# Row-factor products placed later, its low half in another pool, keys' root seeded on ScalarE, decay rows in fewer writes: an encoder trunk on one core

## The chip, the cores and the metric

One of a Trainium2 chip's cores runs the whole kernel in one launch. The metric is device time in microseconds (us), the median of several runs; lower is better. TensorE (PE) multiplies matrices into PSUM banks, VectorE (DVE) and ScalarE (ACT) work on tiles of 128 partitions, GpSimd (POOL) does a few additions, and SyncE (SP) issues the DMAs.

## The reference, cut to what matters

The reference is a bidirectional encoder trunk of two layers on 512 tokens of 1024 features:

```python
for i in range(DEPTH):                                   # DEPTH = 2
    h = h + 0.5 * swiglu(rmsnorm(h, ffn1_norm[i]), ffn1_w_gu[i], ffn1_w_down[i])
    hn = rmsnorm(h, mix_norm[i])
    if i % N_MIXERS == 0: h = h + ssd_mixer(hn, ...)     # state-space mixer, two directions
    else:                 h = h + neighbourhood_attention(hn, ...)
    h = h + 0.5 * swiglu(rmsnorm(h, ffn2_norm[i]), ffn2_w_gu[i], ffn2_w_down[i])
    gate = jax.nn.sigmoid(rmsnorm(h, ple_norm[i]) @ ple_w_gate[i])
    h = h + gate * rmsnorm(p[i] @ ple_w_proj[i], ple_post_norm[i])
```

`rmsnorm(x, g)` is `x * rsqrt(mean(x*x) + 1e-6) * g`; its row factor, the `rsqrt`, is one number per token. `swiglu` has 2816 hidden features (22 tiles of 128), the attention has 16 heads of 64 with a root mean square of each head's query and key, and the mixer has 32 heads with decays that are running sums along the tokens.

## The kernel before, in words

Activations lie transposed, features on the partitions and the 512 tokens along the free axis, so `h` is 8 tiles of 128x512. Every operand is split into a rounded high part and the remainder, and a product of two tiles is three matmuls: L282 (high weight, high activation), L285 (high weight, low activation), L286 (low weight, high activation). I call the three matmuls of one 128-row tile of the contraction a pair; a gemm over 1024 features is 8 pairs, that is 24 matmuls of 512 columns. The later part of each feed-forward (FFN) stage uses blocks of seven products on half tiles, 256 columns wide (L501 to L503); `sums` prepares their inputs from the normalised activations, on DVE and ACT.

Weights arrive in the order of one list: SP loads a unit into a `wr` buffer (L208, 4 buffers), ACT casts the high part (L225, `wh`, 3 buffers), DVE subtracts for the low part (L227, `wl`, 3 buffers). `unit()` hands out one that is ready and prepares the list's next. `ahead(norm)` prepares four more entries behind the row factor's low half.

A norm runs beside the gemm that needs it. `Norm.prep` splits `h[k]` times the gain without the row factor, since that is one number per token and can be applied to the gemm's result. Meanwhile ACT squares `h[k]` (L332) and POOL or DVE adds the squares (L336). `SumSq.begin` then makes the row factor: a high part of the sum (L341, ACT) and a low part (L342, DVE), both from the pool `sq` of 4 buffers; two matmuls of 128x512 with a constant matrix, the wide products (L345, L346), which add over the partitions and spread the sum; logarithm, exponential and square on ACT (L348 to L350), the first two each with an ACT_TABLE_LOAD; and one Newton step on DVE (L351, L352), whose result R lies in the pool `rt` of 3 buffers. There are eleven such places. In the FFN of the first layer's first half (`first`), R is begun between two plain gemms; in each second FFN (FFN2) `side_by_side` runs gate and up of f = 0 together, holding back pair 7 of both, and `begin` stands after pair 4 of up (`at=4`); in the second layer's first FFN it stands behind both gemms (`at=8`). Before R is used, the next gate gemm runs four pairs (`c = 4`). When R is there, DVE forms gate times R (L433) and up times R (L436), ACT takes Silu (L434), DVE multiplies (L437), and `sums` begins with h times R (L455).

The mixer's front computes decay rows on PE, copies them (L727) and their exponentials (L728) to one tile, and SP writes them to DRAM as `crow` and `vrow`: 8 DMAs each of 32x128, in turn (L731, L732). From `crow` one head's row is read back to all partitions (`hs<-crow`, L790), ACT makes its decay matrix from it (L793, L796), and behind that on ACT stand the convolution's copies (L745) that DVE goes on with (L749).

In attention the keys' root (8x512, one row per head of a half) is computed twice, near and far, by `newton_rsqrt` on DVE: 2 integer operations and 3 times 3 others (L317 to L323). DVE also adds the bias to scores (L1274) and takes maxima (L1277); PE turns the result over (L1298) and multiplies it with the values (L1307).

The order of the instructions on each engine is fixed when the program is built: a scheduler takes them mostly in program order by what they need, and `issue_after` ties some behind others.

Of the kernel before, what the change touches and what calls it, by code (L numbers as in the profile page):

```python
# [70 lines left out]
def trunk(ctx, tc, A, out):  # L71
# [30 lines left out]
    def xa(dt=F32R):  # L102
        return md(dt)

    def rt():
        return bp.tile([P, T], F32, name=nm("rt"), tag="rt", bufs=3)

    def bank(tag, bufs):
        return ps.tile([P, T], F32, name=nm("ps"), tag=tag, bufs=bufs)
# [176 lines left out]
            gemm.last = te.matmul(out=pt, lhsT=lo[:, sl], rhs=part(xp, 0, cols), start=False,  # L286
                                  stop=last and k == n - 1)

    def side_by_side(pts, pairs, mid=None, at=4):

        ws = [unit() for _ in pts]
        k = len(pairs) - 1
        for pt, w in zip(pts, ws):
            c = min(at, k) if mid and pt is pts[-1] else k
            gemm(pt, w, pairs[:c], last=False)
            if mid and pt is pts[-1] and at <= k:
                mid()
            if c < k:
                gemm(pt, w, pairs[c:k], first=False, last=False, off=c)
        for pt, w in zip(pts, ws):  # L300
            gemm(pt, w, pairs[k:], first=False, off=k)
        if mid and at > k:
            mid()

# [10 lines left out]
    def newton_rsqrt(m, y, a):  # L315
# [7 lines left out]
            last = v.scalar_tensor_tensor(out=y, in0=a, scalar=1.5, in1=y, op0=ALU.add, op1=ALU.mult)  # L323
        return last

    class SumSq:
        def __init__(self):
            self.acc = None
# [8 lines left out]

        def begin(self, scale=1.0, eps=EPS):

            hi, lo = sq(F32R), sq(F32R)  # L340
            s.copy(out=hi, in_=self.acc)  # L341
            self.last = v.scalar_tensor_tensor(out=lo, in0=self.acc, scalar=eps * D / (scale * P), in1=hi,  # L342
                                               op0=ALU.add, op1=ALU.subtract)
            pt = px_bank()
            te.matmul(out=pt, lhsT=mean[scale], rhs=hi, start=True, stop=False)  # L345
            te.matmul(out=pt, lhsT=mean[scale], rhs=lo, start=False, stop=True)  # L346
            y, a = rt(), self.acc
            s.activation(out=y, in_=pt, func=AF.Ln)  # L348
            s.activation(out=y, in_=y, func=AF.Exp, scale=-0.5)
            s.activation(out=a, in_=y, func=AF.Square)  # L350
            v.scalar_tensor_tensor(out=a, in0=a, scalar=-0.5, in1=pt, op0=ALU.mult, op1=ALU.mult)  # L351
            v.scalar_tensor_tensor(out=y, in0=a, scalar=1.5, in1=y, op0=ALU.add, op1=ALU.mult)  # L352
            self.y = y

        def end(self):
            return self.y
# [1 line left out]
    class Norm:  # L358
# [18 lines left out]
        def begin(self, half=False):  # L377
            if half:
                self.ss.begin(4.0, 4.0 * EPS)
            else:  # L380
                self.ss.begin()

        def end(self):
            return self.ss.end()


    def ffn(norm, nxt, between=None, first=None, at=4):
# [9 lines left out]
        def gate_up(f):  # L397
            pg = mm_bank()
            if not (first and R[0] is None and f == 2):
                pu = mm_bank()  # L400
            if first and f < 2:
                held.append((f, pg, pu))
                if f == 1:
                    first([p for x in held for p in x[1:]], norm.pairs)
                    mid()
                return
            if f == 0 and not first:
                side_by_side((pg, pu), norm.pairs, mid, at)
                held.append((f, pg, pu))
                return  # L410
            if R[0] is None:

                w, c = unit(), 4
                gemm(pg, w, norm.pairs[:c], last=False)
                R[0] = norm.end()
                gemm(pg, w, norm.pairs[c:], first=False, off=c)
                while held:
                    activate(*held.pop(0))
                sums(left.pop(0))
                if first:  # L420
# [126 lines left out]
        for what, *a in ffn_order(chunks):  # L547
            if what == "plain":
                if left and R[0] is not None:
                    sums(left.pop(0))  # L550
                gate_up(a[0])
            elif what == "block":

                if between and a in ([chunks[-1][0] // 2, 0], [NF // 2 - 1, 4]):
                    next(between)
                block(*a)
            elif what == "between":
                made = between and next(between)
            else:
                c, d = a  # L560
                last = c == len(chunks) - 1
                pt = mm_bank() if last else px_bank()
                gemm(pt, unit(last and d == KD - 1), [mids[f] for f in range(*chunks[c])])
                v.scalar_tensor_tensor(out=h[d], in0=pt, scalar=0.5, in1=h[d], op0=ALU.mult, op1=ALU.add)
                if last:
                    nxt(d)
                    if d in (2, 4) and made is not None:
                        made[d // 2]()
        return made and made[0]


    def ple_proj(l):
# [27 lines left out]
            for n in range(KD):  # L600
                pp[n] = (pp[n], r3)

        yield pp, (lambda: ss.begin(4.0, 4.0 * EPS)), finish

    def ple(l, norm, pp, nxt):
        halves = (slice(0, T // 2), slice(T // 2, T))
# [15 lines left out]
        for n in range(KD):  # L622
# [7 lines left out]
                    (sy, s)[x].dma_start(out=out[:, n, cs], in_=h[n][:, cs])  # L630
                continue
            pt = mm_bank()
            gemm(pt, unit(n == KD - 1), norm.pairs, behind=n == 0)
            if n == 0:
                norm.begin(half=True)
                held = pt
# [10 lines left out]
    def ssd(norm, nxt):  # L647
# [11 lines left out]
        gemm(ptd, unit(), norm.pairs)  # L659
        norm.begin()  # L660
        pt0, w0 = mm_bank(), unit()
        gemm(pt0, w0, norm.pairs[:5], last=False)
        R = norm.end()
        gemm(pt0, w0, norm.pairs[5:], first=False, off=5)

        keep = md()
        dtk = keep[:, 0, :].rearrange("p (c k) -> p c k", c=NC)
# [10 lines left out]
        for k in range(KD):  # L678
            t = t2()
            v.scalar_tensor_tensor(out=t, in0=hk[k], scalar=col(norm.gain + k), in1=R, op0=ALU.mult, op1=ALU.mult)  # L680
            xn.append(md(F32R))
            split(xn[k], t, None)

        def steps():

# [43 lines left out]
            for dr in range(2):  # L729
                for c in range(NC):  # L730
                    sy.dma_start(out=crow[dr, :, c * P:(c + 1) * P], in_=rowt[c * 32:(c + 1) * 32, dr * P:(dr + 1) * P])  # L731
                    sy.dma_start(out=vrow[dr, :, c * P:(c + 1) * P],  # L732
                                 in_=rowt[c * 32:(c + 1) * 32, 256 + dr * P:256 + (dr + 1) * P])

        ydram = dp.tile([16, P, T], F32, name="ydram")
        ss = SumSq()
# [292 lines left out]

        for i, cur in enumerate(project(0)):  # L1030
            if i == 2:
                steps()
        e0 = [expo(0, 0)]

        def count(gi, i):
            if gi == NG - 1:
# [42 lines left out]
        ss.begin(0.5, 4.0 * EPS)  # L1079
        for d in range(KD):  # L1080
            pt, w = mm_bank(), unit(d == KD - 1)
            gemm(pt, w, prs[:4], last=False)
            if d == 0:
                r2 = ss.end()
            old = sc()
            sy.dma_start(out=old, in_=hd[d])
            gemm(pt, w, prs[4:], first=False, off=4)

            h[d] = hs()
            u = t2()  # L1090
# [17 lines left out]
    def attention(norm, nxt):  # L1108
# [24 lines left out]
        def keys(js):  # L1133
# [3 lines left out]
            for j in js:  # L1137
# [9 lines left out]
                if j == 2:  # L1147

                    w = unit()
                    gemm(pt, w, norm.pairs[:4], last=False)  # L1150
                    R = norm.end()
                    gemm(pt, w, norm.pairs[4:], first=False, off=4)
                else:
                    gemm(pt, unit(), norm.pairs)
                if j == 4:
# [21 lines left out]
                m, rk, ra = sc(), sc(), sc()  # L1177
                v.tensor_scalar(out=m[:8], in0=kst[:8], scalar1=EPS, scalar2=None, op0=ALU.add)
            yield
            newton_rsqrt(m[:8], rk[:8], ra[:8])  # L1180
            rkd = dp.tile([8, T], F32, name=nm("rkd"))
            sy.dma_start(out=rkd, in_=rk[:8])
            yield
# [376 lines left out]
```

## Time and profile before

| | before |
|---|---|
| median of 3 runs | 2300.32 us (2300.14 to 2300.46) |
| profiled execution | 2300.35 us |
| its span | 2298.5 us, so 1.85 us lie around it |
| PE busy | 2280.6 us, 99% |
| DVE busy | 1829.9 us, 80% |
| ACT busy | 1228.2 us, 53% |
| granted TensorE clock | 1.0 |

A row of the timeline gives start, duration, engine, source line, operation, output and inputs, shape and count; in brackets stands how long the engine sat idle before it and what ended that. Ends of matmuls are modelled: those of 512 columns show some 0.39 us each, but start about 0.23 us apart, so PE loses time wherever two starts lie farther apart than that; the bracket shows about 0.16 us less than is lost. The stages in the trace, from the rows of their lines: first FFN 0 to 360 us, mixer to 893, second FFN to 1257, gated embedding to 1306; in the second layer first FFN to 1645, attention to 1890, second FFN to 2253, embedding to 2298.

### The profile page before, as it was taken

The page shows a single profiled execution, that of the slowest core. Times are in us where ns is not written, and L with a number is a line of the kernel's source. Part 1 is how long each engine was busy: PE and PEld are TensorE (multiplying, and loading weights), DVE is VectorE, ACT ScalarE, POOL GpSimd, SP SyncE. Part 2 cuts the span into 40 slices and gives each one's busy share as a digit, 9 for nine tenths or more (in the row PEclk, how much of TensorE's full clock was granted, in tenths as well). Part 3 has the DMA queues.
Part 4 walks back from the last instruction along what each step waited for, and adds up shares of the span by engine and source line. Part 5 has one row for each costly group of instructions (what it writes and reads, how often), then busy time and mean ns, then how long its engine had stood idle before and what let it go on. Part 6 is the DMA issues. An engine that isn't in the chain of part 4 may idle for free.

```text
span 2298.5 us, 35082 instructions
## 1 busy us (share of the span) xinstructions
PE 2280.6 (99%) x13578; PEld 2008.7 (87%) x13578; DVE 1829.9 (80%) x2522; ACT 1228.2 (53%) x2098; POOL 322.2 (14%) x261
## 2 busy tenths in 40 slices
PE   9999999999999999999999999999999999999999
PEld 7999997888888888899998789999878888999987
DVE  8878868887878959987875897887578869878856
ACT  6433445777677775444446544444546755444453
POOL 0000001355555641000003100000120010000020
PEclk9999999999999999999999999999999999999999
DMA  5323323444444543323223222232557732333222
GB/s 194 116 75 110 106 81 126 161 155 139 144 140 147 186 167 120 106 97 103 88 89 108 101 101 97 92 106 77 168 178 221 228 113 91 111 106 101 82 81 90
DMA packets 105223, 281.68 MB, mean 123 GB/s; under 512 B 13136, under 2 KB 14032, under 8 KB 105056
## 3 DMA queue, kind: packets, MB, share of 16 engines
q1 hardware_dynamic: 104768, 279.30, 36.7%
q8 instruction: 106, 1.74, 0.3%
q14 instruction: 61, 0.50, 0.1%
q10 hardware_dynamic: 288, 0.14, 0.0%
HBM read 259.70 MB, written 13.40 MB: 119 GB/s over the span
## 4 chain that ended last, share of the span: by engine, by line
PE 89%; DVE 6%; ACT 2%; issue 1%; DMA 1%; SPq 0%; POOL 0%; DVEq 0%; POOLq 0%; ACTq 0%
PE ps L282 17%; PE ps L286 17%; PE ps L285 17%; PE ps L503 10%; PE ps L502 10%; PE ps L501 10%; DVE wl L227 1%; PE ps L923 1%; PE ps L882 1%; PE ps L1264 1%; PE ps L903 1%; PE ps L1318 1%; PE ps L838 1%; PE ps L827 1%; ACT wh L225 1%
## 5 line engine op out<-in xcount | busy, mean ns | idle before, releaser
L282 PE MATMUL ps<-md,wh 128*128 128x512 f32 (+1 forms) x2032 | 796.8, 392 | 1.7 <-DVE t L749 1.6
L286 PE MATMUL ps<-md,wl 128*128 128x512 f32 (+1 forms) x2032 | 790.5, 389 | 3.1 <-DVE wl L227 3.1
L285 PE MATMUL ps<-md,wh 128*128 128x512 f32 (+1 forms) x2032 | 791.3, 390 | 0.3 <-DVE md L311 0.3
L225 ACT CAST wh<-wr 128x1024 fp32r<-128x1024 f32 (+2 forms) x395 | 351.4, 892 | 425.8 <-PE ps L285 234.5
L227 DVE TENSOR_TENSOR wl<-wr,wh 128x1024 fp32r<-128x1024 f32 (+2 forms) x395 | 418.5, 1062 | 90.9 <-ACT wh L225 88.3
L286 PEld LDWEIGHTS ps<-md,wl 128*128 128x128 f32 x2032 | 381.5, 188 | 86.2 <-DVE wl L227 6.1
L282 PEld LDWEIGHTS ps<-md,wh 128*128 128x128 f32 x2032 | 382.2, 188 | 76.6 <-issue 2.4
L285 PEld LDWEIGHTS ps<-md,wh 128*128 128x128 f32 x2032 | 382.3, 188 | 73.2 <-DVE md L311 1.0
L225 ACT CAST wh<-md 128x1024 fp32r<-128x1024 f32 x175 | 183.5, 1049 | 318.1 <-PE ps L502 300.4
L336 POOL TENSOR_TENSOR sq<-sq,sq 128x512 f32<-128x512 f32 x71 | 98.9, 1393 | 1635.2 <-ACT sq L332 1315.6
L502 PE MATMUL ps<-md,wh 128*128 128x256 f32 x980 | 277.4, 283 | 0.8 <-DVE md L465 0.8
L501 PE MATMUL ps<-sc,wh 128*128 128x256 f32 x980 | 276.9, 283 | 0.8 <-ACT wh L225 0.8
L503 PE MATMUL ps<-sc,wl 128*128 128x256 f32 x980 | 277.4, 283 | 0.1
L503 PE MATMUL ps<-md,wl 128*128 128x256 f32 x980 | 277.3, 283 | 0.0
L502 PE MATMUL ps<-sc,wh 128*128 128x256 f32 x980 | 277.3, 283 | 0.0
L501 PE MATMUL ps<-md,wh 128*128 128x256 f32 x980 | 277.2, 283 | 0.0
L507 DVE TENSOR_TENSOR t<-ps,t 128x512 f32<-128x512 f32 x245 | 165.8, 689 | 137.7 <-PE ps L503 137.2
L227 DVE TENSOR_TENSOR wl<-md,wh 128x1024 fp32r<-128x1024 f32 x175 | 213.4, 1220 | 16.2 <-ACT wh L225 16.1
L501 PEld LDWEIGHTS ps<-sc,wh 128*128 128x128 f32 x980 | 187.7, 192 | 4.8 <-ACT wh L225 1.0
L502 PEld LDWEIGHTS ps<-sc,wh 128*128 128x128 f32 x980 | 187.7, 192 | 3.8
L502 PEld LDWEIGHTS ps<-md,wh 128*128 128x128 f32 x980 | 188.0, 192 | 2.2 <-DVE md L465 1.0
L501 PEld LDWEIGHTS ps<-md,wh 128*128 128x128 f32 x980 | 188.0, 192 | 1.2
(217 smaller groups left out, 2916.8 us busy)
## 6 DMA issues: line engine op xcount, KB each, us to landing
wr<-in_w_gw_dram SPq DMA_DIRECT2D x70, 512.0 KB, 3.6
md<-in_w_gw_dram SPq DMA_DIRECT2D x70, 512.0 KB, 4.6
wr<-in_w_in_dram SPq DMA_DIRECT2D x65, 512.0 KB, 3.5
wr<-in_w_dn_dram SPq DMA_DIRECT2D x128, 256.0 KB, 2.6
wr<-in_w_gu_dram SPq DMA_DIRECT2D x32, 512.0 KB, 3.5
hs<-crow SPq DMA_DIRECT2D x64, 256.0 KB, 3.7
wr<-in_w_dn_dram SPq DMA_DIRECT2D x32, 384.0 KB, 3.1
wr<-in_w_qkv_dram SPq DMA_DIRECT2D x24, 512.0 KB, 3.6
```

The lines of the kernel that those rows point to most:

```text
L225: splits.append(s.copy(out=hi[:, :n], in_=raw[:, :n]))
L227: v.tensor_sub(out=lo[:, :n], in0=raw[:, :n], in1=hi[:, :n])
L282: m = te.matmul(out=pt, lhsT=hi[:, sl], rhs=part(xp, 0, cols), start=first and k == 0, stop=False)
L285: te.matmul(out=pt, lhsT=hi[:, sl], rhs=part(xp, 1, cols), start=False, stop=False)
L286: gemm.last = te.matmul(out=pt, lhsT=lo[:, sl], rhs=part(xp, 0, cols), start=False, stop=last and k == n - 1)
L336: (v if fast else g).tensor_add(out=self.acc, in0=self.acc, in1=q)
L501: te.matmul(out=o, lhsT=hi[:, sl], rhs=xh, start=j == 0 and kk == 0, stop=False)
L502: te.matmul(out=o, lhsT=hi[:, sl], rhs=xl, start=False, stop=False)
L503: te.matmul(out=o, lhsT=lo[:, sl], rhs=xh, start=False, stop=j == 1 and kk == 3)
L507: v.tensor_add(out=k[to], in0=pt, in1=k[other])
L827: te.transpose(out=pt[:, cs(i)], in_=src[:, cs(c)], identity=ident)
L838: te.matmul(out=pt[:, cs(c)], lhsT=bt[:, dr, cs(c)], rhs=ct_[:, dr, cs(c)], start=True, stop=True)
```

## The change

`SumSq.begin` now makes only the two halves of the sum, and the low half takes a buffer of `rt` instead of `sq`. The two wide products and all behind them become a step of its own, `spread`, which callers place. The root's five instructions become a helper, `seeded_rsqrt`, which the keys' root now uses too, in place of `newton_rsqrt`. The decay rows go out in 4 DMAs of 32x2x128 for `crow` and 4 for `vrow`, all of `crow` first. In the mixer's front one weight split is taken up at k = 5 of the loop over the normalised tiles.

```diff
-    def side_by_side(pts, pairs, mid=None, at=4):
+    def side_by_side(pts, pairs, mid=None, at=4, then=None):
...
         for pt, w in zip(pts, ws):
             gemm(pt, w, pairs[k:], first=False, off=k)
+            if then and pt is pts[0] and at <= k:
+                then()
...
+    def seeded_rsqrt(m, y, a):
+
+        s.activation(out=y, in_=m, func=AF.Ln)
+        s.activation(out=y, in_=y, func=AF.Exp, scale=-0.5)
+        s.activation(out=a, in_=y, func=AF.Square)
+        v.scalar_tensor_tensor(out=a, in0=a, scalar=-0.5, in1=m, op0=ALU.mult, op1=ALU.mult)
+        v.scalar_tensor_tensor(out=y, in0=a, scalar=1.5, in1=y, op0=ALU.add, op1=ALU.mult)
...
-            hi, lo = sq(F32R), sq(F32R)
-            s.copy(out=hi, in_=self.acc)
-            self.last = v.scalar_tensor_tensor(out=lo, in0=self.acc, scalar=eps * D / (scale * P), in1=hi,
+            self.scale, self.hi, self.lo = scale, sq(F32R), rt(F32R)
+            s.copy(out=self.hi, in_=self.acc)
+            self.last = v.scalar_tensor_tensor(out=self.lo, in0=self.acc, scalar=eps * D / (scale * P), in1=self.hi,
                                                op0=ALU.add, op1=ALU.subtract)
+
+        def spread(self):
+
             pt = px_bank()
-            te.matmul(out=pt, lhsT=mean[scale], rhs=hi, start=True, stop=False)
-            te.matmul(out=pt, lhsT=mean[scale], rhs=lo, start=False, stop=True)
...
+            for k, x in enumerate((self.hi, self.lo)):
+                te.matmul(out=pt, lhsT=mean[self.scale], rhs=x, start=k == 0, stop=k == 1)
+            self.y = rt()
+            seeded_rsqrt(pt, self.y, self.acc)
...
-                side_by_side((pg, pu), norm.pairs, mid, at)
+                side_by_side((pg, pu), norm.pairs, mid, at, norm.spread)
...
-                w, c = unit(), 4
+                w, c = unit(), 1
                 gemm(pg, w, norm.pairs[:c], last=False)
+                if first or at > len(norm.pairs) - 1:
+                    norm.spread()
                 R[0] = norm.end()
...
-                    if d in (2, 4) and made is not None:
-                        made[d // 2]()
+                    if 1 < d < 5 and made is not None:
+                        made[d - 1]()
...
-        yield pp, (lambda: ss.begin(4.0, 4.0 * EPS)), finish
+        yield pp, (lambda: ss.begin(4.0, 4.0 * EPS)), ss.spread, finish
...
+            if k == 5:
+                prep_next()
...
+            lines(crow, 0)
+            return lambda: lines(vrow, 256)
...
             if i == 2:
-                steps()
+                late_lines = steps()
         e0 = [expo(0, 0)]
+        late_lines()
...
-            newton_rsqrt(m[:8], rk[:8], ra[:8])
+            seeded_rsqrt(m[:8], rk[:8], ra[:8])
```

`lines(to, x)` issues, for each of the 4 chunks, one DMA for both directions. The remaining callers (mixer's norm after 2 pairs instead of 5, its inner norm after 2 instead of 4, attention and the embedding after 1) place `spread` in the same manner.

What this does to the order on ACT at the second layer's FFN2. Before, the table load and logarithm follow the cast of the sum (`sq_18864`), and the two weight casts (`wh`) come behind the square:

```order
L341 CAST sq_18864<-sq_18606 128x512
L348 ACT_TABLE_LOAD
L348 ACTIVATE rt_18871<-ps_18868 128x512
L349 ACT_TABLE_LOAD
L349 ACTIVATE rt_18871<-rt_18871 128x512
L350 ACTIVATE sq_18606<-rt_18871 128x512
L225 CAST wh_18825<-wr_18738 128x1024
L225 CAST wh_18903<-wr_18829 128x1024
```

The same stretch of ACT after the change, where L351 is the cast of the sum and L330 to L332 are logarithm, exponential and square:

```order
L351 CAST sq_18844<-sq_18586 128x512
L225 CAST wh_18805<-wr_18718 128x1024
L330 ACT_TABLE_LOAD
L330 ACTIVATE rt_18872<-ps_18869 128x512
L225 CAST wh_18883<-wr_18809 128x1024
L331 ACT_TABLE_LOAD
L331 ACTIVATE rt_18872<-rt_18872 128x512
L332 ACTIVATE sq_18586<-rt_18872 128x512
L447 ACT_TABLE_LOAD
L447 ACTIVATE t_18913<-t_18913 128x512
```

One weight cast moved ahead of the logarithm and one between logarithm and exponential; Silu (L447) moved directly behind the square.

The far keys' root on ACT in attention. Before, a weight cast stands between attention's own instructions (L1221 and L1223 are the query's, L1281 the softmax's exponential):

```order
L1221 ACTIVATE sc_16735<-t_16733 128x512
L1223 CAST hs_16737<-t_16733 128x512
L225 CAST wh_16795<-wr_16547 128x1024
L1281 ACTIVATE sc_16770,sm_16774<-sc_16770,sm_16773 128x256 x2
L1299 COPY md_16686<-ps_16833 128x512
```

After, the root's logarithm, exponential and square (8x512) with their two table loads stand around that cast (L1247, L1249 and L1307 are the L1221, L1223 and L1281 of before):

```order
L1247 ACTIVATE sc_16721<-t_16719 128x512
L1249 CAST hs_16723<-t_16719 128x512
L330 ACT_TABLE_LOAD
L330 ACTIVATE sc_16593<-sc_16592 8x512
L225 CAST wh_16775<-wr_16533 128x1024
L331 ACT_TABLE_LOAD
L331 ACTIVATE sc_16593<-sc_16593 8x512
L332 ACTIVATE sc_16594<-sc_16593 8x512
L1307 ACTIVATE sc_16750,sm_16754<-sc_16750,sm_16753 128x256 x2
```

Six instructions came in ahead of the softmax. DVE at the same place after the change; L1250 is the query's low part (L1224 before), L1300 the bias added to scores (L1274 before), L1303 the maximum, L333 and L334 the root's Newton step on 8x512:

```order
L1250 TENSOR_TENSOR hs_16724<-t_16719,hs_16723 128x512
L227 TENSOR_TENSOR wl_16777<-wr_16533,wh_16775 128x1024
L1300 SCALAR_TENSOR_TENSOR sc_16750<-ps_16740,sm_16621,md_16524 128x256
L333 SCALAR_TENSOR_TENSOR sc_16594<-sc_16594,sc_16592 8x512
L1300 SCALAR_TENSOR_TENSOR sc_16750<-ps_16741,sm_16621,sq_16525 128x256
L334 SCALAR_TENSOR_TENSOR sc_16593<-sc_16594,sc_16593 8x512
L1303 TENSOR_REDUCE sm_16753<-sc_16750 128x2
L1300 SCALAR_TENSOR_TENSOR sc_16762<-ps_16740,sm_16621,md_16524 128x256
```

The two Newton operations stand between the first three L1300, where the eleven operations L317 to L323 were spread over this stretch and the rows behind it before.

More of the change, by code (lines that the diff above doesn't have):

```diff
@@ L103, in xa, with rt @@
         return md(dt)
-    def rt():
-        return bp.tile([P, T], F32, name=nm("rt"), tag="rt", bufs=3)
+    def rt(dt=F32):
+        return bp.tile([P, T], dt, name=nm("rt"), tag="rt", bufs=3)
     def bank(tag, bufs):
@@ L338, in begin @@
         def begin(self, scale=1.0, eps=EPS):
-            hi, lo = sq(F32R), sq(F32R)
-            s.copy(out=hi, in_=self.acc)
-            self.last = v.scalar_tensor_tensor(out=lo, in0=self.acc, scalar=eps * D / (scale * P), in1=hi,
+            self.scale, self.hi, self.lo = scale, sq(F32R), rt(F32R)
+            s.copy(out=self.hi, in_=self.acc)
+            self.last = v.scalar_tensor_tensor(out=self.lo, in0=self.acc, scalar=eps * D / (scale * P), in1=self.hi,
                                                op0=ALU.add, op1=ALU.subtract)
+        def spread(self):
             pt = px_bank()
[L345 to L353, printed above, removed]
+            for k, x in enumerate((self.hi, self.lo)):
+                te.matmul(out=pt, lhsT=mean[self.scale], rhs=x, start=k == 0, stop=k == 1)
+            self.y = rt()
+            seeded_rsqrt(pt, self.y, self.acc)
         def end(self):
@@ L381, in begin, with spread @@
                 self.ss.begin()
+        def spread(self):
+            self.ss.spread()
         def end(self):
@@ L632, in ple @@
             pt = mm_bank()
-            gemm(pt, unit(n == KD - 1), norm.pairs, behind=n == 0)
+            w = unit(n == KD - 1)
+            c = 1 if n == 1 else KD
+            gemm(pt, w, norm.pairs[:c], last=c == KD, behind=n == 0)
+            if n == 1:
+                norm.spread()
+                gemm(pt, w, norm.pairs[c:], first=False, off=c)
             if n == 0:
@@ L661, in ssd @@
         pt0, w0 = mm_bank(), unit()
-        gemm(pt0, w0, norm.pairs[:5], last=False)
+        gemm(pt0, w0, norm.pairs[:2], last=False)
+        norm.spread()
         R = norm.end()
-        gemm(pt0, w0, norm.pairs[5:], first=False, off=5)
+        gemm(pt0, w0, norm.pairs[2:], first=False, off=2)
         keep = md()
@@ L728, in steps, with lines @@
             s.activation(out=rowt[:, 256:], in_=pr[:, :256], func=AF.Exp)
-            for dr in range(2):
+            def lines(to, x):
                 for c in range(NC):
-                    sy.dma_start(out=crow[dr, :, c * P:(c + 1) * P], in_=rowt[c * 32:(c + 1) * 32, dr * P:(dr + 1) * P])
-                    sy.dma_start(out=vrow[dr, :, c * P:(c + 1) * P],
-                                 in_=rowt[c * 32:(c + 1) * 32, 256 + dr * P:256 + (dr + 1) * P])
+                    sy.dma_start(out=to[:, :, cs(c)].rearrange("d h t -> h d t"),
+                                 in_=rowt[c * 32:(c + 1) * 32, x:x + 256].rearrange("h (d t) -> h d t", d=2))
+            lines(crow, 0)
+            return lambda: lines(vrow, 256)
         ydram = dp.tile([16, P, T], F32, name="ydram")
@@ L1081, in ssd @@
             pt, w = mm_bank(), unit(d == KD - 1)
-            gemm(pt, w, prs[:4], last=False)
+            gemm(pt, w, prs[:2], last=False)
             if d == 0:
+                ss.spread()
                 r2 = ss.end()
@@ L1086, in ssd @@
             sy.dma_start(out=old, in_=hd[d])
-            gemm(pt, w, prs[4:], first=False, off=4)
+            gemm(pt, w, prs[2:], first=False, off=2)
             h[d] = hs()
@@ L1149, in keys @@
                     w = unit()
-                    gemm(pt, w, norm.pairs[:4], last=False)
+                    gemm(pt, w, norm.pairs[:1], last=False)
+                    norm.spread()
                     R = norm.end()
-                    gemm(pt, w, norm.pairs[4:], first=False, off=4)
+                    gemm(pt, w, norm.pairs[1:], first=False, off=1)
                 else:
```

## Prediction

> **What bounds the kernel now.** I read the page first, for the busy shares and the chain of work that ended last:
>
> ```profile
> PE 2280.6 (99%) x13578; PEld 2008.7 (87%) x13578; DVE 1829.9 (80%) x2522; ACT 1228.2 (53%) x2098; POOL 322.2 (14%) x261
> PE 89%; DVE 6%; ACT 2%; issue 1%; DMA 1%; SPq 0%; POOL 0%; DVEq 0%; POOLq 0%; ACTq 0%
> ```
>
> TensorE runs nearly through, and the change takes no matmul away. So it can only gain where PE waits, and it loses wherever it makes PE wait anew. Next I looked up PE's timeline at each place that is touched. Undisturbed, two 128x512 products start 0.23 apart, as these two wide products in the second layer's FFN2 do:
>
> ```profile
> 1898.40 0.39 PE L345 MATMUL ps<-sq,mean 128*128 128x512 f32 x1
> 1898.63 0.40 PE L346 MATMUL ps<-sq,mean 128*128 128x512 f32 x1
> ```
>
> At the other places PE does wait. In the first layer's FFN2, at the embedding's projection in both layers, in the mixer and twice in attention:
>
> ```profile
> 899.07 0.39 PE L286 MATMUL ps<-md,wl 128*128 128x512 f32 x1
> 900.07 0.50 PE L345 MATMUL ps<-sq,mean 128*128 128x512 f32 x1 [0.61 <-ACT sq L341]
> 900.79 0.50 PE L346 MATMUL ps<-sq,mean 128*128 128x512 f32 x1 [0.22 <-DVE sq L342]
> ...
> 1233.12 0.39 PE L285 MATMUL ps<-md,wh 128*128 128x512 f32 x1
> 1234.22 0.50 PE L346 MATMUL ps<-sq,mean 128*128 128x512 f32 x1 [0.71 <-DVE sq L342]
> ...
> 2231.96 0.50 PE L346 MATMUL ps<-sq,mean 128*128 128x512 f32 x1 [0.71 <-DVE sq L342]
> ...
> 430.91 0.47 PE L282 MATMUL ps<-md,wh 128*128 128x512 f32 x1 [1.59 <-DVE t L749]
> ...
> 1722.05 0.66 PE L1298 MATMUL ps<-msk,t 128*128 128x128 f32 x4 [0.62 <-DVE sc L1274]
> 1727.14 0.63 PE L1307 MATMUL ps<-msk,sc 128*128 128x128 f32 x4 [0.79 <-DVE sm L1243]
> ```
>
> A bracket shows less than is lost: from 1233.12 to 1234.22 are 1.10, of which 0.23 are the normal distance, so 0.87 are lost where 0.71 is printed. I add these 0.16 to a bracket of PE.
>
> **The change part by part.** I give each term as microseconds on PE's end, first the taken value, then its bounds.
>
> *Embedding's projection, both layers: −0.9 each (−1.1 to −0.8).* The low half waited for a buffer of `sq`; it now lies in `rt`, and the products come one step of d later, so PE finds them ready. What goes is 0.87 at each. R is used two steps on, which hides its lateness.
>
> *First layer's first FFN: +0.65 (0 to +0.7).* Here R follows straight from the products:
>
> ```profile
> 29.80 0.60 ACT L348 ACTIVATE rt<-ps 128x512 f32<-128x512 f32 x1 [1.89 <-PE ps L346]
> 33.03 0.69 DVE L351 SCALAR_TENSOR_TENSOR sq<-sq,ps 128x512 f32<-128x512 f32 x1 [2.17 <-ACT sq L350]
> 52.49 0.50 PE L286 MATMUL ps<-md,wl 128*128 128x512 f32 x1
> ```
>
> ACT waits for PE and DVE for ACT, so one pair more before the products, 3 x 0.23 = 0.7, makes R 0.7 later. Behind it DVE has work without a gap, and PE reaches DVE's weight split (the L286 with its longer 0.50 at 52.49) with nothing to spare. I take nearly all; it is nothing if DVE has slack.
>
> *Mixer's front: −1.6 (−1.8 to −0.5).* The decay rows' DMAs, ACT behind them, and DVE's busy time just before:
>
> ```profile
> 410.61 0.42 SPq L731 DMA_DIRECT2D crow<-sc  x1
> ...
> 417.12 0.42 SPq L790 DMA_DIRECT2D hs<-crow  x1
> ```
> ```profile
> 421.31 1.28 ACT L793 ACTIVATE sc<-hs,md 128x128 f32<-128x128 f32 x4 [3.48 <-DMA hs<-crow]
> ```
> ```profile
> 366.10:404.60 38.50, 37.84 (x59) 1.00 0.23 77
> ```
>
> Fourteen issues lie between the first two rows' starts, so one takes 6.51 / 14 = 0.465. Eight issues fewer bring `hs<-crow` 3.7 forward, and ACT, which sat idle 3.48 for it, comes 3.48 forward. Behind L793 on ACT stand the copies that L749 needs, so L749, on which PE waited 1.59 + 0.16 = 1.75 at 430.91, is early. The moved weight split and norm are worth nothing here: DVE is busy 37.84 of 38.50, and its total is the same. I take most of 1.75; if DVE rather than ACT holds L749, a third is left. SP now issues three `hs<-crow` ahead of the next weight load; the loads lead their casts, so I put nothing on it.
>
> *First layer's FFN2: +1.45 (−1.3 to +1.7).* In front, PE gets back 900.79 − 899.07 − 2 x 0.23 = 1.26, since the products come 12 matmuls (three pairs of up, one of gate) = 2.7 later. But R is what decides:
>
> ```profile
> 901.33 0.60 ACT L348 ACTIVATE rt<-ps 128x512 f32<-128x512 f32 x1
> 904.44 1.99 ACT L225 CAST wh<-wr 128x1024 fp32r<-128x1024 f32 x2
> ```
> ```profile
> 908.96 0.69 DVE L436 TENSOR_TENSOR t<-ps,rt 128x512 f32<-128x512 f32 x1
> ```
> ```profile
> 943.55 0.50 PE L286 MATMUL ps<-md,wl 128*128 128x512 f32 x1
> ```
>
> On ACT one cast L225 stands ahead of the first table load now, and waits for the matmul that frees its buffer, gate's last pair at 902.0 (899.07 + 12 x 0.23 and the matmul's own 0.39, less one start). From there: cast 1.0, load 1.3, logarithm 0.6, cast 1.0, load 1.3, exponential and square 0.65 each, two Newton steps and gate times R 0.7 each: 902.0 + 8.6 = 910.6 for up times R, against 908.96: 1.65 late, though DVE has done its two weight splits (L227) before it. PE at 943.55 waits on DVE's L227 with no slack, so DVE's lag passes on. I take 1.45, since some is lost on the way (below). The gain in front doesn't add: PE only arrives earlier at the same wait. If DVE has slack after all, the 1.26 stays.
>
> *Second layer's FFN2: +2.75 (0 to +3.0).* There is no stall to win, as the first rows showed.
>
> ```profile
> 1899.07 0.60 ACT L348 ACTIVATE rt<-ps 128x512 f32<-128x512 f32 x1 [2.60 <-PE ps L346]
> ```
> ```profile
> 1906.70 0.68 DVE L436 TENSOR_TENSOR t<-ps,rt 128x512 f32<-128x512 f32 x1
> ```
> ```profile
> 1903.00:1945.00 42.00, 41.87 (x69) 1.00 0.26 86
> ```
> ```profile
> 1941.29 0.50 PE L286 MATMUL ps<-md,wl 128*128 128x512 f32 x1
> ```
>
> ACT was waiting for PE and its first table load was done. Now the same chain starts at about 1901.1 (the products' old place plus 2.7): 1901.1 + 8.6 = 1909.7 for up times R, 3.0 later than 1906.70. DVE is busy 41.87 of the next 42.00 and PE meets it at 1941.29 without slack. That lateness costs PE almost in full is what a place shows where R already comes so late, the second layer's first FFN:
>
> ```profile
> 1308.99 0.40 PE L282 MATMUL ps<-md,wh 128*128 128x512 f32 x1
> ...
> 1332.39 0.50 PE L286 MATMUL ps<-md,wl 128*128 128x512 f32 x1 [1.01 <-DVE wl L227]
> ...
> 1345.07 0.39 PE L502 MATMUL ps<-md,wh 128*128 128x256 f32 x1 [0.77 <-DVE md L465]
> ...
> 1351.78 0.39 PE L501 MATMUL ps<-sc,wh 128*128 128x256 f32 x1 [0.83 <-ACT wh L225]
> ```
> ```profile
> 1309.80 1.28 ACT L348 ACT_TABLE_LOAD   x1
> 1311.09 0.60 ACT L348 ACTIVATE rt<-ps 128x512 f32<-128x512 f32 x1
> ```
> ```profile
> 1316.46 0.68 DVE L436 TENSOR_TENSOR t<-ps,rt 128x512 f32<-128x512 f32 x1
> ...
> 1319.95 0.69 DVE L437 TENSOR_TENSOR t<-t,t 128x512 f32<-128x512 f32 x1 [1.16 <-ACT t L434]
> ```
>
> From the next gate gemm's start (1308.99) to up times R are 7.5 there, and DVE waits 1.16 more, and PE loses (1.01 + 0.77 + 0.83) + 3 x 0.16 = 3.1 in three waits. In the second layer's FFN2 that distance is 4.4 before (gate starts 16 starts after 1898.63, at 1902.3) and 7.4 after. So lateness of 4.2 (3.1 and the 1.16) costs 3.1 or somewhat more: three quarters to all. That gives 2.75 and 1.45, and the low ends if DVE catches up.
>
> *Second layer's first FFN: 0 (0 to +0.7).* The same rows: a weight cast before its first table load ends that chain, not the products, so a pair more before them changes nothing; at most it costs that pair, 0.7.
>
> *Keys' root: far +2.4 (−1.7 to +3.1), near 0.* DVE loses nine of eleven operations:
>
> ```profile
> 1716.30 0.60 ACT L1223 CAST hs<-t 128x512 fp32r<-128x512 f32 x1
> ```
> ```profile
> 1721.53 0.47 DVE L1274 SCALAR_TENSOR_TENSOR sc<-ps,sm,md 128x256 f32<-128x256 f32 x1
> ```
> ```profile
> L322 DVE SCALAR_TENSOR_TENSOR sc<-sc,sc 8x512 f32<-8x512 f32 x3 | 2.0, 671 | 0.0
> L1277 DVE TENSOR_REDUCE sm<-sc 128x2 f32<-128x512 f32 x2 | 1.3, 660 | 0.0
> ```
>
> Were that all, both waits of attention, 0.78 + 0.95 = 1.7, would go. But the two Newton steps now wait for ACT, and queued behind them on DVE are the biases L1274 and the maximum, on which PE waits. ACT from 1716.9: load 1.3, logarithm 0.6, weight cast 1.0, load 1.3, exponential and square 0.6 each: 1722.3. DVE then: Newton 0.67, bias 0.47, Newton 0.67, maximum 0.66, and the bias that PE waited for, 0.47, ends at 1725.2, where it ended at 1722.0: +3.1. Of the second wait, 0.95, I let 0.7 go, as five root operations no longer stand between. The near root stands where PE waits for nothing on DVE.
>
> [...]
>
> Mixer's inner norm, the embedding's norm and attention's own: 0; no row shows PE waiting there and R is used later.
>
> **Sum** against the profiled 2300.35 (0.03 above the median, so the same for it): −1.8 + 0.65 − 1.6 + 1.45 + 2.75 + 0 + 2.4 = +3.85; FFN lateness may share some wait with the pair behind it, so I round down to +3.5: **2303.8**. What a measurement of this kernel can tell from no change is 0.2%, 4.6: the bounds are 2295.7 and 2304.9.
>
> **The rivals.** *A, lateness hidden:* R's place doesn't matter since DVE catches up before PE meets it, and the far root frees DVE. Then −1.8 − 1.75 − 1.26 − 1.7 = −6.5: 2293.8. For it: every wait named is in the rows. Against: DVE at 41.87 of 42.00. Chance 0.18.
>
> *B, FFN late, far root good:* ACT finishes the root while DVE has other work; −1.7 instead of +2.4: 2299.7. Against it is the order of DVE behind the two steps. Chance 0.16.
>
> *C, slower:* the Silu behind R. In the second layer's first FFN DVE waited 1.16 for Silu (1319.95). If Silu's table load, now directly behind the late square, ends after DVE's work in between, both FFN2 pay this again: 2303.8 + 2.3 = 2306.1. It decides when Silu ends over two DVE operations (1.4) after up times R starts. Chance 0.15.
>
> [...] Chance 0.03.
>
> That the edits don't happen is excluded by the order on the engines.
>
> **How the numbers follow.** The forecast has 0.48; its own range, from the keys' and FFN bounds, is 2301.5 to 2306, of which 0.14 lies over 2304.9. Faster: A, 0.18. Slower: 0.14 + C 0.15 + D 0.03 = 0.32. Same: 0.34 + B 0.16 = 0.50. The range reaches from 2295 (B with gains in one FFN2) to 2307.5 (C with the far root's upper end) and leaves out A's and D's.
>
> **What would show it.** In the changed trace: the wide products of FFN2 with no wait; up times R at about 910.6 and 1909.7 on before's clock; PE's waits on L227 some 35 us later grown to 1.5 and 2.8; `hs<-crow` 3.7 earlier and no wait at 430.91; DVE idle before L333 until 1722, and PE's L1298 3 later. It would be wrong if DVE has gaps before those waits, or if the Newton step on keys finds its square ready.

## The result and the profile after

The changed kernel takes 2306.44 us in the median of 12 runs (2304.08 to 2307.82), the kernel before 2300.36 (2300.01 to 2300.71). The ratio is 1.0025, 95% interval 1.0016 to 1.0034: slower, by 6.1. The predicted 2303.8 lay 2.6 under it, its range up to 2307.5 holds it, and the lower end of the changed kernel's runs lies 0.3 above the forecast. The median also lies over 2304.9, the end of what the prediction called no change, though the lower end of the interval, 1.0016, lies within the 0.2% that this bound stands for. That the runs spread over 3.7, where the kernel before spreads over 0.7, was not foreseen.

The profiled execution took 2307.35 with a span of 2305.2 and a mean clock of 0.998. To see where PE's time went, I number its 13578 matmuls in order of time, subtract the start of each in the trace before from its start in the trace after, and take the steps of this difference from stage to stage:

| stage (PE's clock before) | predicted | after |
|---|---|---|
| first FFN, to 357 | +0.65 | +0.75 |
| mixer's front, 357 to 405 | 0 | +1.58 |
| mixer, 405 to 860 | −1.6 | −1.84 |
| first layer's FFN2 | +1.45 | −1.35, then +2.61 |
| embedding's projections, two | −0.9 each | −1.06, −1.05 |
| second layer's first FFN | 0 | +0.08 |
| attention | +2.4 | +4.38 |
| second layer's FFN2 | +2.75 | +2.59 |
| sum | +3.85 | +6.69 |

Six rows of eight hold within 0.5. The two that don't, the mixer's front and attention, are 1.58 and 1.98 off, more than the whole gap. In both, PE's timeline has one long wait (rows of 399.17 and 1725.90, of the changed kernel):

```profile
390.82 0.50 PE L286 MATMUL ps<-md,wl 128*128 128x512 f32 x1 [0.62 <-DVE wl L227]
399.17 0.50 PE L286 MATMUL ps<-md,wl 128*128 128x512 f32 x1 [2.16 <-DVE wl L227]
```
```profile
1725.90 1.12 PE L1324 MATMUL ps<-msk,t 128*128 128x128 f32 x4 [3.70 <-DVE sc L1300]
1726.67 0.78 PE L282 MATMUL ps<-md,wh 128*128 128x512 f32 x1
1727.24 0.63 PE L285 MATMUL ps<-md,wh 128*128 128x512 f32 x1
1727.67 0.63 PE L286 MATMUL ps<-md,wl 128*128 128x512 f32 x1
```

Behind the second wait the starts of L285 and L286 are 0.43 apart instead of 0.23. The windows of PE at these two places say why; behind the length, the busy time and its count stands the granted clock, then the transfers' share of the DMA engines and their GB/s:

```profile
398.00:400.00 2.00, 0.83 (x3) 0.95 0.01 4
400.00:402.00 2.00, 2.00 (x6) 0.50 0.74 256
402.00:404.00 2.00, 2.00 (x8) 0.70 0.83 250
404.00:406.00 2.00, 2.00 (x11) 1.00 0.76 256
1722.00:1724.00 2.00, 0.20 (x1) 1.00 0.00 0
1724.00:1726.00 2.00, 0.10 (x1) 0.54 0.04 8
1726.00:1728.00 2.00, 2.00 (x7) 0.50 0.83 281
1728.00:1730.00 2.00, 2.00 (x6) 0.50 0.99 377
1730.00:1732.00 2.00, 2.00 (x11) 0.75 1.06 330
```

Worked out from these means, the clock stands at half for 3.4 us in the mixer and 6.8 in attention, where the fall comes while PE still waits, so that some 5 of them have work. In the kernel before it was 1.00 in the window from 5 to 2298.

The two times named for up times R came as predicted. DVE in the second layer's FFN2 and in the first layer's (its up times R is L449):

```profile
1914.81 0.68 DVE L449 TENSOR_TENSOR t<-ps,rt 128x512 f32<-128x512 f32 x1
...
911.07 0.68 DVE L449 TENSOR_TENSOR t<-ps,rt 128x512 f32<-128x512 f32 x1
```

Less the 5.13 and 0.49 that PE was late by then, these are 1909.7 and 910.6, the two numbers of the forecast. PE pays in three waits on DVE, where a single longer wait on L227 was forecast, here in the first layer:

```profile
938.44 0.39 PE L515 MATMUL ps<-md,wh 128*128 128x256 f32 x1 [0.73 <-DVE md L478]
941.18 0.39 PE L516 MATMUL ps<-sc,wl 128*128 128x256 f32 x1 [0.57 <-DVE wl L227]
...
945.66 0.50 PE L286 MATMUL ps<-md,wl 128*128 128x512 f32 x1 [0.88 <-DVE wl L227]
```

At the far keys' root DVE stood for ACT's square, with the biases behind it; its rows, then ACT's:

```profile
1721.73 0.48 DVE L1300 SCALAR_TENSOR_TENSOR sc<-ps,sm,md 128x256 f32<-128x256 f32 x1
1723.18 0.68 DVE L333 SCALAR_TENSOR_TENSOR sc<-sc,sc 8x512 f32<-8x512 f32 x1 [0.98 <-ACT sc L332]
1723.79 0.47 DVE L1300 SCALAR_TENSOR_TENSOR sc<-ps,sm,sq 128x256 f32<-128x256 f32 x1
1724.19 0.67 DVE L334 SCALAR_TENSOR_TENSOR sc<-sc,sc 8x512 f32<-8x512 f32 x1
1724.79 0.67 DVE L1303 TENSOR_REDUCE sm<-sc 128x2 f32<-128x512 f32 x1
1725.38 0.46 DVE L1300 SCALAR_TENSOR_TENSOR sc<-ps,sm,md 128x256 f32<-128x256 f32 x1
```
```profile
1720.57 1.28 ACT L331 ACT_TABLE_LOAD   x1
1721.86 0.63 ACT L331 ACTIVATE sc<-sc 8x512 f32<-8x512 f32 x1
1722.52 0.63 ACT L332 ACTIVATE sc<-sc 8x512 f32<-8x512 f32 x1
```

The bias that PE waits for ends at 1725.84, or 1725.1 less the 0.77 carried in; 1725.2 was forecast. In the mixer `hs<-crow` went out at 412.97, 4.2 earlier than in the trace before (3.7 was forecast) although PE was 2.3 late there, and the wait at 430.91 is gone.

### The profile page after: what moved, and what is told of

It is laid out like the page before. It is cut to its first block, busy times and chain, and to the rows that moved or that the text cites. A ratio compares the mean times of both kernels' runs of the same rounds, so it can differ in the third digit from the quotient of the medians.

```text
span 2305.2 us, 35067 instructions
## 1 busy us (share of the span) xinstructions
PE 2283.4 (99%) x13578; PEld 2013.8 (87%) x13578; DVE 1824.1 (79%) x2504; ACT 1237.3 (54%) x2108; POOL 324.3 (14%) x261
## 4 chain that ended last, share of the span: by engine, by line
PE 90%; DVE 7%; ACT 1%; issue 1%; DMA 0%; ACTq 0%; DVEq 0%; SPq 0%
PE ps L282 18%; PE ps L286 18%; PE ps L285 18%; PE ps L516 10%; PE ps L515 10%; PE ps L514 10%; DVE wl L227 1%; PE ps L946 1%; PE ps L905 1%; DVE md L310 1%; PE ps L926 1%; PE ps L1290 1%; PE ps L1344 1%; PE ps L861 1%; PE ps L850 1%
## 5 line engine op out<-in xcount | busy, mean ns | idle before, releaser
L286 PE MATMUL ps<-md,wl 128*128 128x512 f32 (+1 forms) x2032 | 791.9, 390 | 6.9 <-DVE wl L227 6.9
L282 PE MATMUL ps<-md,wh 128*128 128x512 f32 (+1 forms) x2032 | 798.2, 393 | 0.1
L285 PE MATMUL ps<-md,wh 128*128 128x512 f32 (+1 forms) x2032 | 792.3, 390 | 0.4 <-DVE md L313 0.3
L227 DVE TENSOR_TENSOR wl<-wr,wh 128x1024 fp32r<-128x1024 f32 (+2 forms) x395 | 417.1, 1058 | 95.0 <-ACT wh L225 93.0
L286 PEld LDWEIGHTS ps<-md,wl 128*128 128x128 f32 x2032 | 382.4, 188 | 90.1 <-DVE wl L227 9.4
L282 PEld LDWEIGHTS ps<-md,wh 128*128 128x128 f32 x2032 | 383.2, 189 | 75.2 <-ACT md L312 0.5
L285 PEld LDWEIGHTS ps<-md,wh 128*128 128x128 f32 x2032 | 383.2, 189 | 73.7 <-DVE md L313 1.1
L227 DVE TENSOR_TENSOR wl<-md,wh 128x1024 fp32r<-128x1024 f32 x175 | 213.6, 1221 | 16.7 <-ACT wh L225 16.6
L515 PEld LDWEIGHTS ps<-md,wh 128*128 128x128 f32 x980 | 188.0, 192 | 4.0 <-DVE md L478 2.8
L516 PEld LDWEIGHTS ps<-sc,wl 128*128 128x128 f32 x980 | 187.7, 192 | 2.5 <-DVE wl L227 2.3
```

Source lines behind the costliest of these rows:

```text
L227: v.tensor_sub(out=lo[:, :n], in0=raw[:, :n], in1=hi[:, :n])
L282: m = te.matmul(out=pt, lhsT=hi[:, sl], rhs=part(xp, 0, cols), start=first and k == 0, stop=False)
L285: te.matmul(out=pt, lhsT=hi[:, sl], rhs=part(xp, 1, cols), start=False, stop=False)
L515: te.matmul(out=o, lhsT=hi[:, sl], rhs=xl, start=False, stop=False)
L516: te.matmul(out=o, lhsT=lo[:, sl], rhs=xh, start=False, stop=j == 1 and kk == 3)
```

## The experiments

My theory: the losses are R's lateness in both FFN2 (2.6 each), the far root's place in DVE's queue (3.1), and the half clock behind PE's two long waits; the gains are the decay rows and the projections. Its rivals: the clock falls by itself; FFN2 loses by the weight casts on ACT rather than by the products' place; what the change gains at one place was only what it lost just before. Each kernel ran with the kernel before on the same chip (its medians there: 2300.84 in the first four, 2300.31 in the next four, 2300.74 in the last three; the ratios are to these). Losses by stage are steps against the trace before, as in the table.

**far_newton.** The far root goes back to DVE, the near one stays:

```diff
-            seeded_rsqrt(m[:8], rk[:8], ra[:8])
+            (newton_rsqrt if js[0] else seeded_rsqrt)(m[:8], rk[:8], ra[:8])
```

> The changed kernel with the far keys' root alone computed by the old eleven DVE operations; the near root stays seeded. Theory (the seeded far root makes PE wait 3.7 us, and that wait then halves TensorE's clock for some 5 us): both go, 4.3 of the changed kernel's loss, so 2306.4 - 4.3 = 2302.1; granted clock 1.00 in the attention stage, PE's first turn of the values back at some 3 us earlier. Rival (the lower clock in that stretch comes by itself, not from the wait): only the wait's 3.1 goes, 2303.3, and the clock stays under 1 in that stretch. If the near root costs anything, it shows as a wait of PE between 1675 and 1700.

Measured: 2302.40, ratio 1.0006 (0.9997 to 1.0015). Attention's +4.38 is 0.00, and PE's waits there are those of before, 0.61 and 0.78. So the far root is the whole loss of attention and the near root costs nothing. A second thing shows. The wait at 399 is still there, as long as in the changed kernel, but in this execution the clock held, and the mixer's front lost −0.02 instead of +1.58:

```profile
399.22 0.50 PE L286 MATMUL ps<-md,wl 128*128 128x512 f32 x1 [2.16 <-DVE wl L227]
```
```profile
398.00:400.00 2.00, 0.78 (x3) 1.00 0.01 4
400.00:402.00 2.00, 2.00 (x10) 1.00 0.73 254
402.00:404.00 2.00, 2.00 (x11) 1.00 0.84 217
```

**fill.** The changed kernel with matmuls by a zero matrix (`zero`, 128x112) added to a running sum where PE waits:

```diff
+    def fill(pt, x, n):
+        for _ in range(n):
+            tc.keep_in_program_order(te.matmul(out=pt[:112], lhsT=zero, rhs=x, start=False, stop=False))
...
+            if k == 0:
+                fill(pt, part(xp, 0, cols), more)      # more = 8 in the mixer's unit of the wait
...
+            if j == 2:
+                fill(pt, part(norm.pairs[3], 0, slice(0, T)), 10)   # in attention
...
```

> The changed kernel with matmuls by a zero matrix (they add zero to a running sum) placed in PE's two longest waits: 8 in the mixer's front, 10 in attention. Nothing else is changed, DVE and ACT are as late as before. Theory (the clock halves because PE stands idle): the granted clock is 1.00 in both stretches, and the time lost behind the waits, some 1.5 in the mixer and 1.2 in attention, goes: 2306.4 - 2.7 = 2303.7. Rival (the clock halves for another reason, such as the transfers in that stretch): the same half clock in the same places, 2306.4 or, if the extra matmuls lie in the way, more.

Measured: 2305.25, ratio 1.0018 (1.0009 to 1.0027). DVE is as late as before, PE still stands until 1725 for the same bias, and the clock is full at both places:

```profile
1721.41 2.26 PE L130 MATMUL ps<-md,zero 128*112 128x512 f32 x9
1725.27 0.66 PE L1335 MATMUL ps<-msk,t 128*128 128x128 f32 x4 [1.60 <-DVE sc L1311]
```
```profile
400.00:402.00 2.00, 2.00 (x10) 1.00 0.79 256
...
1726.00:1728.00 2.00, 2.00 (x10) 1.00 0.93 360
1728.00:1730.00 2.00, 2.00 (x17) 1.00 0.99 399
```

Attention's +4.38 is +2.17, with nothing changed but that PE was less idle. Ten of eleven runs have a mean clock of 1.000, one of 0.999; of the changed kernel's twelve one has 1.000, two 0.999, nine 0.998. So at both places the clock stood at 0.50 behind an idle PE and at 1.00 behind a filled one, and the transfers, as dense as before (shares of 0.79 and 0.93 from 400 and 1726, against 0.74 and 0.83), are not the cause. The expected 2303.7 was missed all the same. Over the kernel before beside it the median is 4.4 later, against 6.1 without the fill, so 1.7 is saved; trace against trace it is 2.84, since the changed kernel's profiled run (2307.35) lies near the top of its runs and this one's (2304.55) is the lowest of its own. Of the 1.5 expected in the mixer only 0.57 came (−0.24 to −0.81 for the front and the stretch behind it), because the added matmuls lie partly in the way there.

**ffn2_now and ffn2_casts.** In the first, `begin` is followed at once by `spread` in both FFN2; in the second the products stay late, but the two weight casts are tied behind the square:

```diff
+            if not first and at <= 7:
+                norm.spread()
...
```
```diff
+        def then():
+            norm.spread()
+            with tc.issue_after(seeded_rsqrt.square.ins):
+                for _ in range(5):
+                    prep_next()
...
```

> The changed kernel with the wide products of both second FFNs back at their old place, straight behind the two halves of the sum. Theory (the products' later place makes R late, DVE's lag passes on to PE some 35 us later): both FFN2 stages return to their old time, 1.26 + 2.61 = 3.9 less: 2302.5. Rival (the loss in these stages is caused by what stands before them, a lag carried in): no change there, 2306.4.

> The changed kernel with the wide products of both second FFNs at the new, late place, but with the two weight casts that now stand ahead of and between logarithm and exponential put back behind the square on ACT, in the old order. Theory (the later place of the products alone makes R late, because the casts then delay the weights instead): no gain or under 0.5, about 2306. Rival (the casts in the chain make R late, 2.0 of the 3.0): R comes 2 earlier, up times R some 2 earlier in the second layer, and the two stages give back up to 1.5 and 2.0: 2303.

Measured: 2302.45, ratio 1.0007 (0.9998 to 1.0017), and 2305.18, ratio 1.0018 (1.0009 to 1.0027). With the products at their old place the two stages lose −0.16 and +0.03: the whole of 1.26 and 2.59 is theirs. With the casts put back, they lose −1.35 + 2.18 and +2.15: the casts in the chain cost 0.43 in each stage, the late place the rest. The rival, that the casts are two thirds of it, fell. The trace says why. R does come earlier (in the second layer L334 starts at 1907.86, or 1905.8 less the 2.11 carried in, against 1908.4 in the changed kernel), but the casts and so the two weight splits are now late and stand between R and its use:

```profile
1908.47 2.35 DVE L227 TENSOR_TENSOR wl<-wr,wh 128x1024 fp32r<-128x1024 f32 x2
1911.34 0.68 DVE L456 TENSOR_TENSOR t<-ps,rt 128x512 f32<-128x512 f32 x1
```

Up times R (L456 here) is at 1909.2 less what was carried in, only 0.45 earlier than in the changed kernel, and the first layer gives the same 0.45. So what PE pays for is the lateness of gate and up times R, whether R or the splits before them are the cause.

**rows_only, proj_only, both_gains.** The kernel before with 4 + 4 row writes; with the low half in `rt` and the projection's `spread` one step of d later; with both. Their edits are those lines of the change.

> The kernel before with one part of the change alone: the decay rows in 4 + 4 writes, crow first. Theory (the wait of 1.59 on L749 at 430.91 goes with the eight issues, as in the changed kernel, where that stretch gains 1.8): 2300.4 - 1.8 = 2298.6, no wait at 430.91. Rival (that gain in the changed kernel was only the time lost to the half clock just before, given back): no gain, 2300.4.

> The kernel before with the low half in the pool rt everywhere and, at the embedding's projection alone, the wide products a step of d later; elsewhere the products stay where they were. Theory (both waits at 1234 and 2232 go): -1.06 and -1.05, 2298.3. Rival (the other pool's three buffers make something else wait, so that not all of it comes): 2299 to 2300.4.

> The kernel before with those two parts together and nothing else of the change. Theory (the gains are at different places and add): 2300.4 - 1.8 - 2.1 = 2296.5, faster than both kernels. Rival (one gain hides in a wait that the other leaves): 2298.

Measured: 2299.54 (0.9997, 0.9988 to 1.0006), 2297.95 (0.9991, 0.9982 to 1.0000), 2297.36 (0.9987, 0.9978 to 0.9996). The projection gives −1.07 and −1.05, all that was expected. The rows give half: the wait at 430.91 is gone, and another came where none had been, on the convolution one unit earlier (L751 here is the L749 of before):

```profile
422.56 0.47 PE L282 MATMUL ps<-md,wh 128*128 128x512 f32 x1 [0.74 <-DVE t L751]
```

ACT's decay matrices (L793 before, L795 here), now early, stand before the convolution's own operations there, and DVE waits for these:

```profile
417.46 0.69 DVE L755 SCALAR_TENSOR_TENSOR md<-t,t 128x512 f32<-128x512 f32 x1 [1.95 <-ACT t L754]
```

This order is read from the rows and was not tested by itself. In trace against trace the rows' stretch gives −0.89 of 1.83. Both gains together are faster than the kernel before by 3.0 (0.13%), which is small but clear of 1 in the interval.

**far_later.** The seeded far root, its two DVE operations and the store taken one step later:

```diff
+            seeded_rsqrt(m[:8], rk[:8], ra[:8], 0)     # ACT's three
+            if js[0]:
+                yield
+            seeded_rsqrt(m[:8], rk[:8], ra[:8], 1)     # DVE's two
...
```

> The changed kernel with the far root's two Newton operations on DVE taken one step later, so that they stand behind the biases and the first maximum; ACT's part stays where it is. Theory (DVE stood blocked at the head of its queue until ACT's square, and PE for DVE): PE's long wait at 1722 shrinks from 3.7 to under 1, the clock stays 1.00 there, attention's +4.4 falls to between -0.5 and +0.5: 2302. Rival (the six instructions on ACT make PE late, not DVE's queue): a wait of 2 to 3 stays, 2305.

Measured: 2309.04, ratio 1.0039 (1.0025 to 1.0052). That is the median of five runs. The first half of the theory held: DVE's queue was the block, PE's wait at 1722 is 0.84 and the clock holds there. But the expected time was wrong, since the root's way to memory and back now ends later under a DVE that waits for it (2.27 before and 3.11 in the changed kernel, where PE loses no more than before; here 6.26):

```profile
1748.37 0.75 DVE L1222 SCALAR_TENSOR_TENSOR sc<-md,gqk,sc 128x512 f32<-128x512 f32 x1 [6.26 <-DMA sc<-rkd]
```
```profile
1749.32 0.66 PE L1340 MATMUL ps<-msk,sc 128*128 128x128 f32 x4 [2.93 <-DVE sm L1276]
1751.59 1.97 PE L1340 MATMUL ps<-msk,sc 128*128 128x128 f32 x8 [1.62 <-ACT md L1332]
```

Attention lost 6.2 in all, 5.9 of it at this wait and behind it, where the clock is low as well: from 1755.07 to 1756.77 L282, L285 and L286 start 0.42 to 0.43 apart, as they do at 0.50 in the changed kernel, and from 1757.55 0.23.

**front_split.** The changed kernel without `prep_next()` at k = 5:

> The changed kernel without the weight split at k = 5 of the mixer's front. Theory (DVE is busy through that front, so the split only moves PE's waiting: early waits are spared and one wait of over 2 us near 399 grows, long enough to halve the clock behind it in most runs): PE waits twice, near 380 and near 399, each under 1.5, the clock stays 1.00 there, and PE is at the same place at 450: 1.0 to 1.6 less in the runs that had lost the clock there, 2305.2. Rival (the split helps in itself): the wait near 380 comes back and nothing else goes, 2306.4 to 2307.5.

Measured: 2304.70, ratio 1.0018 (1.0009 to 1.0026). The wait is split again, and the clock held at both places in the profiled run (1.00 in the windows from 376 to 384 and from 394 to 406):

```profile
379.90 0.50 PE L286 MATMUL ps<-md,wl 128*128 128x512 f32 x1 [0.98 <-DVE wl L227]
398.75 0.50 PE L286 MATMUL ps<-md,wl 128*128 128x512 f32 x1 [1.79 <-DVE wl L227]
```

The second is longer than the 1.5 expected. The front and the stretch behind it give −0.04 − 1.38 = −1.42, against −1.87 with the split when the clock held (far_newton) and −0.24 when it didn't (the changed kernel). So the split is worth 0.45 or costs 1.2, by the clock.

**gains_front, gains_front_fill.** The two gains with the mixer's front of the changed kernel, without and with eight zero matmuls in its wait:

> The kernel of the two gains (decay rows, embedding's projection) with the mixer's front of the changed kernel added: the weight split at k = 5 and the norm's wide products after two pairs. Theory: the wait of 0.9 at 422 that the rows alone left goes, so 0.9 below the two gains, 2296.5, in runs that keep the clock; the one long wait near 398 is over 2 again, and runs that lose the clock there pay 1.6, 2298.1. Rival (the 0.9 at 422 came from the rows' order, not from the front): 2297.4 or more in all runs.

> The same with eight matmuls by a zero matrix in the long wait near 398. Theory (an idle PE is what halves the clock): the clock is 1.00 in every run, and the median is that of the runs before that kept it, 2296.5. Rival: as without them, or later by the eight matmuls' 1.8.

Measured: 2299.17, ratio 0.9994 (0.9985 to 1.0003), and 2298.53, ratio 0.9988 (0.9979 to 0.9997). The wait at 422 is gone as expected, but neither beats the two gains alone. Without the fill the clock fell behind the 2.16 again (0.50 from 400 to 402, +1.62), and in attention PE also lost 2.8 behind a DVE that waited 4.12 for the keys' root at 1744. That wait stands in the other profiles too, between 2.27 and 3.84 long (far_later aside), where PE loses at most 0.2 more than in the kernel before; what makes it longer here stays open. With the fill the front kept its clock (1.00 from 394 to 406), but the eight matmuls lie partly in the way (+0.57 by 405), and what is left, +0.57 − 1.25, is no more than the two gains alone have there, −0.74. So the front brings nothing here that can be measured.

## Why the prediction was right, and where it was not

*Embedding, first FFN, second layer's first FFN:* right within 0.2 each. The first FFN's +0.65 was measured as +0.75. The starts of the executions differ by up to 0.7 in their first 10 us, so the sum up to 357 is worth little by itself, but the step at the place that was named is not: PE now waits there,

```profile
53.23 0.50 PE L286 MATMUL ps<-md,wl 128*128 128x512 f32 x1 [0.84 <-DVE wl L227]
```

and it loses between 0.65 and 0.91 at this split in all seven kernels that have the later products in the first FFN, between −0.02 and 0.11 in the five that don't.

*Both FFN2:* right in mechanism and size. Up times R came at the predicted 910.6 and 1909.7, ffn2_now gave the whole loss back, and the gain in front (−1.35, predicted 1.26) was swallowed as the text said. The estimate that three quarters or more of the lateness reaches PE held: 2.59 of 3.0 (rounding down from the second layer's first FFN), 1.26 of 1.65.

*Far keys' root:* the wait was right (3.1 predicted, 3.85 − 0.77 = 3.08 measured), and the second wait went, 1.0 of it where 0.7 was let go. With the clock kept, in fill, the stage loses +2.17 beside the predicted +2.4. What failed is a term put at nothing: the sum has none for the clock behind the first wait, which cost the other 2.2. The wait in the queue was foreseen, that its length had a price of its own was not.

*Mixer's front:* the step "The moved weight split and norm are worth nothing here" failed. Its ground was right: DVE is busy there and its total is the same, so PE's waiting is the same in sum. But before, PE waited three times, 0.23, 0.92 and 1.17 as printed; now it waits 0.62 and 2.16, and the clock falls to 0.50 behind the last. Two kernels show both outcomes of the same wait: +1.58 with the fall, −0.02 without. The rows' −1.6 was measured as −1.84, but rows_only shows that the rows alone are worth 0.9; the other half came with the new front only (−1.87 in far_newton, where the clock held).

*Rivals:* A and B fell with the far root and the lags. C didn't happen: behind the late R, DVE's multiplication by Silu (L450, 1917.07) has no wait. The 0.03 of D stands for a cost of a table load beyond its own length, which no run shows: the load at 1720.57 takes 1.28, and the exponential starts 0.01 behind its end.

Summing up, the sum was +3.85, and without the clock's two losses the trace has 6.69 − 1.6 − 2.2 = +2.9. The one run of the changed kernel with a clock of 1.000 took 2304.08, beside the predicted 2303.8. That the range holds the median is in part luck: its upper end, 2307.5, stood for rival C, which didn't happen, and what filled that room was the clock, which no term and no rival of the prediction has.

## What to carry to other kernels

PE's waits that the moved split took away in front of DVE, which was busy 37.84 of 38.50 there, came back where the two met next and in one piece (0.23, 0.92 and 1.17 became 0.62 and 2.16): look for that point and its length before counting a gain. Behind the one piece of 2.13 to 2.16 the clock fell in four profiles of six; behind the two of front_split (0.98 and 1.79) it held at 1.00. Before half of a step goes to another engine, count what is queued behind the half that then waits: behind the far root's Newton step stood the bias that PE needed, 3.08 later than before. Where a step is moved later, take its whole chain of dependents along, and ask which engine will stand at its end: in far_later DVE stood there 6.26.

## What the runs showed of the hardware

While PE had work, TensorE's granted clock stood at 0.50 twice in the changed kernel's trace, from 399.80 to 403.21 and from 1724.17 to 1731.00, that is for 3.41 and 6.83, and at 1.00 from 403.21 to 1724.17 and from 1731.00 to 2300. Worked out from the means of the windows, the low stretches are as long elsewhere: 3.4 from 400.2 in ffn2_now, 3.4 from 399.7 and from 1748.0 in gains_front.

The length of a wait alone did not decide. These are PE's waits as printed, and the clock in the windows behind them:

| kernel, place | PE's waits | clock behind them |
|---|---|---|
| changed, mixer's front | 2.16 | 0.50 |
| gains_front, mixer's front | 2.16 | 0.50 |
| ffn2_now, mixer's front | 2.13 | 0.55, 0.59 |
| far_later, mixer's front | 2.13 | low: starts 0.42 to 0.43 apart from 399.30 |
| far_newton, mixer's front | 2.16 | 1.00 |
| ffn2_casts, mixer's front | 2.15 | 1.00 |
| front_split, mixer's front | 1.79 | 1.00 |
| fill, mixer's front | 0.75 | 1.00 |
| changed, attention | 3.70 | 0.50 |
| gains_front, attention | 0.33, 1.15 | 0.75, 0.83 (windows of 4 us) |
| fill, attention | 1.60 | 1.00 |
| far_newton, attention | 0.61, 0.78 | 1.00 |

Where the clock fell, I also added up by how much matmuls start farther apart than undisturbed (0.23 for 512 columns): in the changed kernel that is 2.44 of the 3.41 ahead of the fall at 399.80, in ffn2_now 2.07 of the 3.41 ahead of its fall at 400.21. In ffn2_casts, where the clock held behind the 2.15, the same sum is 0.83 from 393.96 to 397.37 and 1.59 from 397.37 to 400.78. Its own fall comes at 1725.16, a whole number of steps of 3.41 later (389); the two falls of the changed kernel and of ffn2_now lie 388 such steps apart, those of gains_front 395. That the same wait goes both ways by where it lies among such steps is my reading of these traces. It was not shown: no kernel was built to move a wait, and far_newton has no fall in its windows from which steps could be counted.

The runs of the changed kernel spread with their mean clock: 2304.08 at 1.000, 2304.82 and 2305.25 at 0.999, 2305.46 to 2307.82 at 0.998. With products that add zero in PE's waits the clock kept 1.00 at both places in fill, and in gains_front_fill in every window from 0 to 2250.
